# Turning the softmax probabilities of four heads by VectorE block transposes and small transfers instead of TensorE transposes, in one decoder layer on one core

## The chip, the cores and the metric

The kernel runs on one core of a Trainium2 chip. The metric is device time in microseconds (us) of one execution. Before the change, three runs gave 305.89 us in the median (305.8 to 306.62). A profiled execution is a run of its own with its own time.

## The reference

One layer of a hybrid decoder trunk on a sequence of 256 tokens with model width 1024, all in float32:

- RMSNorm of x, then one combined input projection. Its columns are the queries, keys and values of 8 attention heads of width 64, and the queries, keys, values, output gate and decay gate of 4 gated-linear-attention heads.
- The attention heads (called MoBA): rotary embedding, then causal softmax attention. A block is 256 keys long and there are 256 tokens, so there are no past blocks to choose from and each query attends causally to its own block.
- The linear-attention heads: a chunked scan, normalised per head and multiplied by silu of the gate.
- Both halves side by side go through the output projection, and x is added.
- Then RMSNorm, an up-projection to 2 x 2816, a causal depthwise convolution of width 3, silu gating, a down-projection, the residual and a last RMSNorm.

## The kernel before, in words

TensorE does every large product in three passes: each float32 operand is split into a rounded part `hi` and a rest `lo`, and the kernel adds hi x hi, hi x lo and lo x hi. ScalarE makes `hi` (line 99), VectorE makes `lo = raw - hi` (line 102). Weights come through a ring of four raw buffers. `split_lo` (line 101) calls `load_next` when a slot of weights is fully split, so the load of a later slot is issued by SyncE (SP) right behind that subtraction.

The input projection is a list of 48 numbered steps (line 121). From step 24 on, a step is one contraction block of 128 for a group of 512 columns and both token halves: six matrix products of 512 columns. Steps 24 to 31 make the values of attention, 32 to 39 those of the linear heads, 40 to 47 the output gate; the output projection follows as steps 48 to 63. Weight slots 12 and 13 serve steps 32 to 39, slots 14 and 15 serve steps 40 to 47 (two steps to each half of a slot), slots 16 to 19 the output projection.

All other work is written out by hand in a table (lines 631 to 653): for a step, or for the middle of a step (36.5 is between the two token halves of step 36), it lists the calls that are emitted there. TensorE, ScalarE and VectorE each run their instructions strictly in the order in which they are emitted; SyncE and GpSimd run theirs in order too. So a call placed in the table at one step stands in one place in three or four queues.

The attention heads are done in pairs, one pair per "visit", at steps 29, 33.5, 36.5 and 40. A visit of pair `pr` has these parts:

- `m_scores(pr)` (line 526): TensorE makes the scores of both heads in two PSUM tiles, and with them one level of the linear heads (`lvl_c`).
- `m_max(h)` (line 553): VectorE adds the causal mask, writes into a 448-wide tile `pe` and takes the maximum of each row. Columns 0 to 127 of a head's tile belong to its first 128 queries, columns 128 to 383 to its last 128, with 64 queries in each half of the rows (in the second group the two halves are swapped).
- `m_exp(h)` (line 561): ScalarE takes the exponential and its row sum.
- `m_div(h)` (line 568): VectorE takes the reciprocals, ScalarE scales the 128 columns of the first part, VectorE the 256 of the second.
- `m_pt(pr)` (line 574): one visit later, TensorE turns the probabilities of the pair with 12 transposes into PSUM, and ScalarE copies them out to `pt` with four instructions (lines 587 and 588).

At step 45.5 everything comes together: `m_pt(3)`, the last level of the linear heads (`lvl_last`, copied out by ScalarE in `lvl_last_d`), `m_av(0)` (heads 0 to 3 times values, line 591), `m_av(1)` (heads 4 to 7), and `g_av(0)`, `g_av(1)` for the linear heads. Then steps 46 and 47 finish the projection, `g_tail` at step 48 normalises the linear heads, and `g_out` at step 51 transposes them on TensorE.

Late in the kernel the same idea as in the change is already used once: `blocks` (line 910) turns 32 x 32 blocks on VectorE and `to_rows` (line 916) puts the blocks in their places with 16 transfers from the SP queue.

Of the kernel before, what the change touches and what calls it, by code (L numbers as in the profile page):

```python
# [26 lines left out]
NG = 256 + RANK + 256  # L27
# [7 lines left out]
def trunk_kernel(ctx: ExitStack, tc: tile.TileContext, xT_d, wG_d, w5_d, wo_d, up_d, dn_d,  # L35
                 par_d, gla_g_d, fin_g_d, wgu_d, cos_d, sin_d, causal_d, lvl_d, ident_d, out_d):
    nc = tc.nc
    V, A, T, DMA = nc.vector, nc.scalar, nc.tensor, nc.sync
# [123 lines left out]
    ml = main.tile([128, KT, S], F32R, name="ml")  # L162
# [43 lines left out]

    ap_ = ctx.enter_context(ExitStack())
    at = ap_.enter_context(tc.tile_pool(name="attn", bufs=1))
    gqk = at.tile([128, 2, NG], F32, name="gqk")
    gqT = at.tile([128, 2, S], F32, name="gqT")  # L210
    gkT = at.tile([128, 2, S], F32, name="gkT")
    gk1 = at.tile([128, 2, S], F32, name="gk1")
    q1 = at.tile([128, 256], F32, name="q1")
    dec = [at.tile([128, 512 >> i], F32, name=f"dec{i}") for i in range(7)]
    q128 = at.tile([128, 2, 64], F32, name="q128")
    k128 = at.tile([128, 2, 64], F32, name="k128")
    ATd = at.tile([128, 8, 64], F32, name="ATd")
    AT = at.tile([128, 8, 128], F32, name="ATf")
    AT01 = at.tile([128, 4, 128], F32, name="AT01")
    wgs = at.tile([128, 256], F32R, name="wgs")  # L220
    lrs = at.tile([128, 2, 8, RANK], F32R, name="lrs")
    lrT = at.tile([128, S], F32R, name="lrT")
# [6 lines left out]
    gv = at.tile([128, 2, 512], F32, name="gv")  # L229
# [8 lines left out]
    st = {}  # L238
# [198 lines left out]
        st["last"] = p  # L437

    def lvl_last_d():
        for h in range(2):  # L440
            p = st["last"][h]
            for a in range(2):
                A.activation(AT.rearrange("p (a g h) t -> p a g h t", a=2, h=2)[0:64, a, :, h, 64:128],
                             p[HALVES[a], 0:128].rearrange("p (g t) -> p g t", g=2), AF.Copy)
            A.activation(AT01.rearrange("p (a h) t -> p a h t", h=2)[:, :, h],
                         p[:, 128:384].rearrange("p (a t) -> p a t", a=2), AF.Copy)
# [7 lines left out]
    def g_av(tt):  # L454
        p = att()
        for h in range(HG):
            pr, hh = divmod(h, 2)
            o = p[:, h * DV:(h + 1) * DV]
            vs = slice(h * DV, (h + 1) * DV)
            if tt == 1:  # L460
                T.matmul(o, AT01[:, pr * 2 + hh], gv[:, 0, vs], start=True, stop=False)
            i = (pr * 2 + tt) * 2 + hh
            T.matmul(o, AT[:, i], gv[:, tt, vs], start=(tt == 0), stop=True)  # L463
        st["o", tt] = p
# [81 lines left out]

    pes = [at.tile([128, 448], F32, name=f"pe{i}") for i in range(4)]
    for pe in pes:  # L550
        nc.gpsimd.memset(pe[64:128, 384:448], 0.0)

    def m_max(h):
        p, pe = st["s", h], pes[h % 4]
        mx = at.tile([128, 8], F32, name="mx", bufs=4)
        for i, (a, b, c) in enumerate(((0, 128, 0), (64, 320, 128))):
            V.tensor_tensor_reduce(pe[:, c:c + b - a], p[:, a:b], causal[:, c:c + b - a], -(HD ** -0.5), 3e38,
                                   ALU.add, ALU.min, mx[:, i:i + 1])
        st["mx", h] = mx

    def m_exp(h):
        pe, mx = pes[h % 4], st["mx", h]
        for i, (a, b) in enumerate(((0, 128), (128, 384))):
            A.activation(pe[:, a:b], pe[:, a:b], AF.Exp, bias=mx[:, i:i + 1], scale=-1.0,
                         accum_out=mx[:, 4 + i:5 + i])
        st["pe", h] = pe

    def m_div(h):
        mx, pe = st["mx", h], st["pe", h]
        V.reciprocal(mx[:, 6:8], mx[:, 4:6])  # L570
        A.activation(pe[:, 0:128], pe[:, 0:128], AF.Copy, scale=mx[:, 6:7])
        V.tensor_scalar(pe[:, 128:384], pe[:, 128:384], mx[:, 7:8], None, op0=ALU.mult)

    def m_pt(pr):

        p = [att() for _ in range(2)]
        for h in range(2):
            for c in range(3):
                for r, rs in enumerate(HALVES):
                    a = c * 128 + 64 * (r and c > 0)  # L580
                    T.transpose(p[r][:, (3 * h + c) * 64:(3 * h + c) * 64 + 64],  # L581
                                st["pe", 2 * pr + h][rs, a:a + 128], ident[rs, rs])
        pt = at.tile([128, 2, 384], F32, name="pt", bufs=4)
        for r in range(2):
            o = pt.rearrange("p h (c t) -> p h c t", c=3)
            i = p[r][:, :384].rearrange("p (h c t) -> p h c t", h=2, c=3)
            A.activation(o[:, :, 0, HALVES[r]], i[:, :, 0], AF.Copy)
            A.activation(o[:, :, 1:, HALVES[1 - r]], i[:, :, 1:], AF.Copy)
        st["pt", pr] = pt

    def m_av(n):

        p = att()
        for pr in (2 * n, 2 * n + 1):
            c = S * (pr % 2)
            for hh in range(2):
                h = 2 * pr + hh
                pt = st["pt", pr][:, hh]
                r = slice(64 * hh, 64 * hh + 64)
                vs = slice(64 * h, 64 * h + 64)  # L600
                T.matmul(p[r, c:c + S], mv[:, 0, vs], pt[:, 0:256], start=True, stop=False, skip_group_check=True)  # L601
                T.matmul(p[r, c + 128:c + 256], mv[:, 1, vs], pt[:, 256:384],
                         start=False, stop=True, skip_group_check=True)
        mh = st["mh"]
        pv = p.rearrange("p (a t) -> p a t", a=2)
        A.activation(mh[:, 2 * n:2 * n + 2], pv, AF.Copy)
        V.tensor_sub(ml[:, 2 * n:2 * n + 2], pv, mh[:, 2 * n:2 * n + 2])


    plan = {}  # L610
# [20 lines left out]
    for q, f in (  # L631
# [78 lines left out]
    for q, (g, k) in enumerate(steps):  # L710
# [6 lines left out]
        n, kk = where[g, k]  # L717
        h_, l_ = slots[n].view(512 if g else NG)
        if g in (1, 2):
            for pr in range(4):  # L720
# [3 lines left out]
                o = st[names[g]][pr // 2][:, (pr % 2) * S:(pr % 2 + 1) * S]  # L724
# [39 lines left out]
    for q in range(48, 64):  # L764
        ph, j = divmod(q - 48, 8)
# [409 lines left out]
```

## Time and profile before

| | |
|---|---|
| Median of three runs | 305.89 us (305.8 to 306.62) |
| The profiled execution's own time | 306.11 us |
| Span of its instructions | 304.1 us |
| TensorE busy | 297.7 us (98%) |
| VectorE busy | 248.2 us (82%) |
| ScalarE busy | 207.0 us (68%) |
| GpSimd busy | 4.8 us (2%) |

The span runs from the first to the last instruction of the program; 2.0 us of the execution's own time lie outside it. Busy shares are averages over the whole span. Steps 33.5 to 48, where the change is made, lie at 57 to 91 us of it. In the rows of the trace the first number is the start in us from the beginning of the span and the second the duration; "L581" is line 581 of the kernel; "x12" counts instructions that were merged in one row, and "[0.64 <-ACT hi L99]" says that the engine stood idle for 0.64 us before the row until that instruction released it.

### The profile page before, as it was taken

To read this page: it belongs to the slowest core of one execution; us is meant where nothing else is said; L and a number is where in the kernel's file an instruction comes from. 1 tells how busy PE (TensorE), PEld (TensorE's weight loads), DVE (VectorE), ACT (ScalarE), POOL (GpSimd) and SP (SyncE) were. 2 spreads that over 40 slices of the span, in tenths; PEclk is the share of its full clock that TensorE was granted. 3 is DMA by queue.
4 is the path that set the end of the run, shared out by engine and by line. 5 is a ranking of instruction groups with operands and counts; after the bars stand their busy time and mean duration, and the time that the engine had idled before them with its cause. 6 is when DMAs were issued, how large, how long until landed. Compare 5 with 4: busy or idle time off the path is not lost.

```text
span 304.1 us, 6224 instructions
## 1 busy us (share of the span) xinstructions
PE 297.7 (98%) x2470; PEld 282.2 (93%) x2470; DVE 248.2 (82%) x464; ACT 207.0 (68%) x384; POOL 4.8 (2%) x21
## 2 busy tenths in 40 slices
PE   8999999999999999999999999999999999999992
PEld 8999988777889999999999999999999999999992
DVE  3788998999387699799999998887888788876653
ACT  3988999898998487657667775555556665534362
POOL 2020000000000000000000000000000000000000
PEclk9999999999999999999999999999999999999999
DMA  6998845274553542991567666448788622220003
GB/s 163 391 332 307 297 165 198 91 261 141 176 182 134 204 168 65 426 370 32 210 245 256 254 235 236 170 156 224 211 194 234 267 71 69 71 69 2 0 0 139
DMA packets 20892, 56.38 MB, mean 185 GB/s; under 512 B 9840, under 2 KB 11648, under 8 KB 16640
## 3 DMA queue, kind: packets, MB, share of 16 engines
q1 hardware_dynamic: 20720, 55.86, 53.1%
q8 instruction: 19, 0.31, 0.4%
q10 hardware_dynamic: 144, 0.13, 0.1%
q14 instruction: 9, 0.07, 0.1%
HBM read 53.89 MB, written 1.05 MB: 181 GB/s over the span
## 4 chain that ended last, share of the span: by engine, by line
PE 98%; ACT 0%; issue 0%; DVE 0%; ACTq 0%
PE att L116 14%; PE att L117 14%; PE att L118 14%; PE acc L116 14%; PE acc L118 14%; PE acc L117 14%; PE att L746 4%; PE acc L727 1%; PE att L77 1%; PE att L399 1%; PE att L535 1%; PE att L581 1%; PE att L463 1%; PE att L601 1%; PE acc L735 1%; PE att L302 0%
## 5 line engine op out<-in xcount | busy, mean ns | idle before, releaser
L99 ACT ACTIVATE hi<-raw 128x1024 fp32r<-128x1024 f32 (+4 forms) x87 | 79.9, 941 | 38.4 <-PE att L117 31.9
L102 DVE TENSOR_TENSOR lo<-raw,hi 128x1024 fp32r<-128x1024 f32 (+4 forms) x89 | 93.6, 1065 | 14.0 <-ACT hi L99 14.0
L116 PE MATMUL att<-hh,hi 128*128 128x256 f32 x352 | 98.4, 279 | 0.0
L117 PE MATMUL att<-hl,hi 128*128 128x256 f32 x352 | 98.3, 279 | 0.0
L118 PE MATMUL att<-hh,lo 128*128 128x256 f32 x352 | 98.2, 279 | 0.0
L116 PEld LDWEIGHTS att<-hh,hi 128*128 128x128 f32 x352 | 66.2, 188 | 0.0
L117 PEld LDWEIGHTS att<-hl,hi 128*128 128x128 f32 x352 | 66.2, 188 | 0.0
L118 PEld LDWEIGHTS att<-hh,lo 128*128 128x128 f32 x352 | 66.2, 188 | 0.0
L873 DVE SCALAR_TENSOR_TENSOR c<-us,par,c 128x256 f32<-128x256 f32 x88 | 40.7, 482 | 4.1 <-ACT c L865 2.5
L865 ACT ACTIVATE c<-us,par 128x256 f32<-128x256 f32 x44 | 24.0, 591 | 23.7 <-DVE us L855 18.4
L118 PE MATMUL acc<-dhi,gl 128*128 128x512 f32 (+1 forms) x88 | 32.1, 365 | 0.0
L117 PE MATMUL acc<-dlo,gh 128*128 128x512 f32 (+1 forms) x88 | 32.1, 365 | 0.0
L116 PE MATMUL acc<-dhi,gh 128*128 128x512 f32 (+1 forms) x88 | 31.9, 363 | 0.0
L815 DVE TENSOR_TENSOR dlo<-draw,dhi 128x1024 fp32r<-128x1024 f32 x22 | 26.6, 1218 | 0.0
L855 DVE TENSOR_TENSOR us<-att,rb 128x512 f32<-128x512 f32 x20 | 13.8, 688 | 11.5 <-PE att L118 11.5
L810 ACT ACTIVATE dhi<-draw 128x1024 fp32r<-128x1024 f32 x22 | 23.0, 1046 | 0.0
L116 PE MATMUL acc<-hi,ah 128*128 128x512 f32 x48 | 19.5, 406 | 0.0
L118 PE MATMUL acc<-hi,al 128*128 128x512 f32 x48 | 19.0, 396 | 0.0
L117 PE MATMUL acc<-lo,ah 128*128 128x512 f32 x48 | 19.0, 396 | 0.0
L117 PEld LDWEIGHTS acc<-dlo,gh 128*128 128x128 f32 x88 | 16.5, 188 | 2.0
L116 PEld LDWEIGHTS acc<-dhi,gh 128*128 128x128 f32 x88 | 16.5, 188 | 1.9
L118 PEld LDWEIGHTS acc<-dhi,gl 128*128 128x128 f32 x88 | 16.5, 188 | 1.9
(222 smaller groups left out, 511.0 us busy)
## 6 DMA issues: line engine op xcount, KB each, us to landing
raw<-in_up SPq DMA_DIRECT2D x22, 1024.0 KB, 4.9
draw<-in_dn SPq DMA_DIRECT2D x22, 512.0 KB, 5.7
raw<-in_w SPq DMA_DIRECT2D x7, 1024.0 KB, 6.8
raw<-in_wo SPq DMA_DIRECT2D x4, 1024.0 KB, 4.8
raw<-in_w SPq DMA_DIRECT2D x4, 512.0 KB, 5.6
raw<-in_wG SPq DMA_DIRECT2D x3, 528.0 KB, 5.8
raw<-in_w SPq DMA_DIRECT2D x4, 256.0 KB, 5.4
xg<-hB SPq DMA_DIRECT2D x16, 64.0 KB, 6.4
```

Of the source, the lines that this page charges most:

```text
L77: T.matmul(wp[:, :w], zero, zero[:, :w], start=True, stop=True)
L99: A.activation(self.hi[:, a:b], self.raw[:, a:b], AF.Copy)
L102: V.tensor_sub(self.lo[:, a:b], self.raw[:, a:b], self.hi[:, a:b])
L116: T.matmul(out, sh, mh, start=first, stop=False, **kw)
L117: T.matmul(out, sh, ml, start=False, stop=False, **kw)
L118: T.matmul(out, sl, mh, start=False, stop=last, **kw)
L746: T.matmul(st["G"][tt][c][:, :c1 - c0], sta[:, k, tt * 128:(tt + 1) * 128], mov[:, kk, c0:c1], start=k == 0 and i == 0, stop=k == KT - 1 a ...
L810: A.activation(hi, downs[i][0], AF.Copy)
L815: V.tensor_sub(lo, d, hi)
L855: V.tensor_tensor(u[:, :, 2:], upo[i][2].rearrange("p (a t) -> p a t", a=2), rb[:, None, :].to_broadcast([128, 2, S]), op=ALU.mult)
L865: A.activation(cv[i][:, a], u[:, a, 2:], AF.Identity, bias=par[:, P_CB + m:P_CB + m + 1], scale=par[:, P_CW + 2 * 2 * NP + m:P_CW + 2 * 2 ...
L873: V.scalar_tensor_tensor(c[:, a], u[:, a, w:w + S], par[:, wc:wc + 1], c[:, a], op0=ALU.mult, op1=ALU.add)
```

## The change

Heads 0 to 3 no longer go through `m_pt`. Their four probability tiles become one tile `pe4`. Once the third visit has issued its work, `p_blocks` transposes all 32 x 32 blocks of `pe4` with two VectorE instructions into `tb`, which takes the memory of `gqk`; the second instruction overwrites, for token rows 64 to 127, the blocks whose order differs. Then `p_turn` places the blocks in `pt4` with twenty transfers, taken in turn by the SP queue and the GpSimd queue: 12 that move 32 x 12 pieces of 128 bytes and 8 that move 32 x 4. `m_av(0)` reads `pt4`.

What goes with it: heads 4 and 5 use two buffers of another tile group (`e`), heads 6 and 7 the first two quarters of `pe4` again. For heads 2 to 5 the second scaling of `m_div` moves from VectorE to ScalarE. `m_pt(0)` and `m_pt(1)` are gone. At step 36.5, `lo(14, 1)` now comes behind `lvl_d_(4)`, `p_blocks` and `p_turn`. `lo(15, 0)` moves from step 37 to the fourth visit, behind `m_exp(7)`, and the fourth visit moves from step 40 to 40.5. The columns of `m_av(0)` come out in another order, so its copies (ScalarE) and subtractions (VectorE) are three instructions each instead of one. `AT01` takes the memory of `gk1`, and `pt` needs two buffers instead of four.

```diff
-    gqk = at.tile([128, 2, NG], F32, name="gqk")
+    gqk = at.tile([128, 2, NG], F32, name="gqk", tag="gqk")
...
-    pes = [at.tile([128, 448], F32, name=f"pe{i}") for i in range(4)]
-    for pe in pes:
-        nc.gpsimd.memset(pe[64:128, 384:448], 0.0)
+    pe4 = at.tile([128, 4, 448], F32, name="pe4")
+    nc.gpsimd.memset(pe4[64:128, :, 384:448], 0.0)
+
+    def pe_of(h):
+        if h not in (4, 5):
+            return pe4[:, h % 4 if h < 4 else h - 6]
+        if ("pe", h) not in st:
+            st["pe", h] = at.tile([128, 512], F32, name="e", bufs=2)
+            nc.gpsimd.memset(st["pe", h][64:128, 384:448], 0.0)
+        return st["pe", h]
+
+    pt4 = at.tile([128, 12, 128], F32, name="pt4")
+    nc.gpsimd.memset(pt4.rearrange("p (h c) t -> p h c t", c=3)[64:128, :, 2, 64:128], 0.0)
+
+    def p_blocks():
+        st["tb"] = at.tile([128, 50, 32], F32, name="tb", tag="gqk")
+        t = st["tb"][:, 0:48].rearrange("p (h n) b -> p h (n b)", h=4)
+        V.transpose(t, pe4[:, :, 0:384])
+        V.transpose(t[64:128, :, 64:192], pe4[64:128, :, 0:128])
+
+    def p_turn():
+        n = 0
+        for b in range(4):
+            j = b // 2
+            for k in range(4):
+                src = st["tb"][32 * b:32 * b + 32]
+                dst = pt4[32 * k:32 * k + 32, :, 32 * b:32 * b + 32]
+                o = k + 2 * j
+                whole = j == 0 or k < 2
+                for c in ((None,) if whole else (0, 1)):
+                    q = (DMA, nc.gpsimd)[n % 2]
+                    n += 1
+                    if c is None:
+                        q.dma_start(dst, src[:, o:o + 45:4])
+                    else:
+                        q.dma_start(dst[:, c::3], src[:, o + 4 * c:o + 4 * c + 37:12])
...
-        V.tensor_scalar(pe[:, 128:384], pe[:, 128:384], mx[:, 7:8], None, op0=ALU.mult)
+        if h in (2, 3, 4, 5):
+            A.activation(pe[:, 128:384], pe[:, 128:384], AF.Copy, scale=mx[:, 7:8])
+        else:
+            V.tensor_scalar(pe[:, 128:384], pe[:, 128:384], mx[:, 7:8], None, op0=ALU.mult)
...
-                pt = st["pt", pr][:, hh]
+                pt = pt4[:, 3 * h:3 * h + 3].rearrange("p c t -> p (c t)") if n == 0 else st["pt", pr][:, hh]
...
-        A.activation(mh[:, 2 * n:2 * n + 2], pv, AF.Copy)
-        V.tensor_sub(ml[:, 2 * n:2 * n + 2], pv, mh[:, 2 * n:2 * n + 2])
+        for a, b, c in ((0, 256, 0),) if n else ((0, 128, 0), (128, 192, 192), (192, 256, 128)):
+            A.activation(mh[:, 2 * n:2 * n + 2, a:b], pv[:, :, c:c + b - a], AF.Copy)
+        for a, b, c in ((0, 256, 0),) if n else ((0, 128, 0), (128, 192, 192), (192, 256, 128)):
+            V.tensor_sub(ml[:, 2 * n:2 * n + 2, a:b], pv[:, :, c:c + b - a], mh[:, 2 * n:2 * n + 2, a:b])
...
-            (33.5, lambda: do((hi, 13, 1), (m_scores, 1), (m_pt, 0), (m_max, 2), (m_exp, 2), (m_max, 3), (m_exp, 3), (lvl_u, 4), (m_div, 2), (m_div, 3), (lo, 13, 1), (lvl_d_, 3), (mv_evac, 0), (mv_evac, 1), (hi, 14, 0), (lo, 14, 0))),
-            (36.5, lambda: do((hi, 14, 1), (m_scores, 2), (m_pt, 1), (m_max, 4), (m_exp, 4), (m_max, 5), (m_exp, 5), (lvl_u, 5), (m_div, 4), (m_div, 5), (lo, 14, 1), (lvl_d_, 4))),
-            (37, lambda: do((hi, 15, 0), (lo, 15, 0))),
-            (40, lambda: do((hi, 15, 1), (m_scores, 3), (m_pt, 2), (m_max, 6), (m_exp, 6), (m_max, 7), (m_exp, 7), (lvl_u64,), (lvl_d_, 5), (m_div, 6), (m_div, 7), (lvl_join,), (lo, 15, 1))),
+            (33.5, lambda: do((hi, 13, 1), (m_scores, 1), (m_max, 2), (m_exp, 2), (m_max, 3), (m_exp, 3), (lvl_u, 4), (m_div, 2), (m_div, 3), (lo, 13, 1), (lvl_d_, 3), (mv_evac, 0), (mv_evac, 1), (hi, 14, 0), (lo, 14, 0))),
+            (36.5, lambda: do((hi, 14, 1), (m_scores, 2), (m_max, 4), (m_exp, 4), (m_max, 5), (m_exp, 5), (lvl_u, 5), (m_div, 4), (m_div, 5), (lvl_d_, 4), (p_blocks,), (p_turn,), (lo, 14, 1))),
+            (37, lambda: do((hi, 15, 0))),
+            (40.5, lambda: do((hi, 15, 1), (m_scores, 3), (m_pt, 2), (m_max, 6), (m_exp, 6), (m_max, 7), (m_exp, 7), (lo, 15, 0), (lvl_u64,), (lvl_d_, 5), (m_div, 6), (m_div, 7), (lvl_join,), (lo, 15, 1))),
```

More of the change, by code (lines that the diff above doesn't have):

```diff
@@ L208, in trunk_kernel @@
     at = ap_.enter_context(tc.tile_pool(name="attn", bufs=1))
-    gqk = at.tile([128, 2, NG], F32, name="gqk")
+    gqk = at.tile([128, 2, NG], F32, name="gqk", tag="gqk")
     gqT = at.tile([128, 2, S], F32, name="gqT")
     gkT = at.tile([128, 2, S], F32, name="gkT")
-    gk1 = at.tile([128, 2, S], F32, name="gk1")
+    gk1 = at.tile([128, 2, S], F32, name="gk1", tag="gk1")
     q1 = at.tile([128, 256], F32, name="q1")
@@ L218, in trunk_kernel @@
     AT = at.tile([128, 8, 128], F32, name="ATf")
-    AT01 = at.tile([128, 4, 128], F32, name="AT01")
     wgs = at.tile([128, 256], F32R, name="wgs")
@@ L439, in lvl_last_d @@
     def lvl_last_d():
+        AT01 = st["AT01"] = at.tile([128, 4, 128], F32, name="AT01", tag="gk1")
         for h in range(2):
@@ L460, in g_av @@
             if tt == 1:
-                T.matmul(o, AT01[:, pr * 2 + hh], gv[:, 0, vs], start=True, stop=False)
+                T.matmul(o, st["AT01"][:, pr * 2 + hh], gv[:, 0, vs], start=True, stop=False)
             i = (pr * 2 + tt) * 2 + hh
@@ L545, in masks @@
             nc.gpsimd.tensor_copy(causal[rs, 320:384], causal[rs, rs])
-    pes = [at.tile([128, 448], F32, name=f"pe{i}") for i in range(4)]
-    for pe in pes:
-        nc.gpsimd.memset(pe[64:128, 384:448], 0.0)
+    pe4 = at.tile([128, 4, 448], F32, name="pe4")
[30 more added lines that the diff above has]
+                        q.dma_start(dst[:, c::3], src[:, o + 4 * c:o + 4 * c + 37:12])
     def m_max(h):
-        p, pe = st["s", h], pes[h % 4]
+        p, pe = st["s", h], pe_of(h)
         mx = at.tile([128, 8], F32, name="mx", bufs=4)
@@ L561, in m_exp @@
     def m_exp(h):
-        pe, mx = pes[h % 4], st["mx", h]
+        pe, mx = pe_of(h), st["mx", h]
         for i, (a, b) in enumerate(((0, 128), (128, 384))):
@@ L582, in m_pt @@
                                 st["pe", 2 * pr + h][rs, a:a + 128], ident[rs, rs])
-        pt = at.tile([128, 2, 384], F32, name="pt", bufs=4)
+        pt = at.tile([128, 2, 384], F32, name="pt", bufs=2)
         for r in range(2):
```

## The prediction

> **What bounds the kernel now.** I read the page's busy shares first, then the chain of work that ended last, then the queues of TensorE, VectorE and ScalarE in order of time from 57 to 96 us, and last the transfers.
>
> ```profile
> span 304.1 us, 6224 instructions
> PE 297.7 (98%) x2470; PEld 282.2 (93%) x2470; DVE 248.2 (82%) x464; ACT 207.0 (68%) x384; POOL 4.8 (2%) x21
> PE 98%; ACT 0%; issue 0%; DVE 0%; ACTq 0%
> ```
>
> TensorE is busy for 98% and the chain runs through it from start to end: whatever leaves its queue is gained, as long as nothing that its later instructions wait for comes late. The chain in order of time shows the pieces that the change touches, and that TensorE waits nowhere between them:
>
> ```profile
> 58.57 0.53 PE att L581 x12
> 64.65 0.53 PE att L581 x12
> 71.97 0.43 PE acc L116
> 72.40 0.23 PE acc L117
> 79.87 0.52 PE att L581 x12
> 81.25 0.59 PE att L601 x4
> 82.76 0.43 PE att L601 x4
> 84.06 1.09 PE att L463 x8
> 94.63 0.64 PE att L499 x16
> ```
>
> A product of 512 columns takes 0.23 us, so a step of six takes 1.4 us. `m_pt(0)` and `m_pt(1)` are the first two rows. `m_pt(3)` stands at 79.87, `m_av(0)` at 81.25, `m_av(1)` at 82.76, `g_av(0)` at 84.06, `g_out` at 94.63.
>
> **The change, part by part.** *TensorE* loses 24 transposes: 2 x 0.53 = **-1.06 us**. The scores and the reorderings change nothing in its count. All its work from the third visit on comes 1.06 us earlier if it never waits: `m_pt(3)` at 78.81, `m_av(0)` at 80.2, `m_av(1)` at 81.7, `g_av(0)` at 83.0, `g_out` at 93.6.
>
> *VectorE and ScalarE* must then deliver earlier. VectorE's queue in order of time:
>
> ```profile
> 62.02 0.35 DVE L572 TENSOR_SCALAR pe<-pe,mx 128x256 f32<-128x256 f32 x1
> 65.01 1.23 DVE L102 TENSOR_TENSOR lo<-raw,hi 128x1024 fp32r<-128x1024 f32 x1 [0.64 <-ACT hi L99]
> 68.21 0.35 DVE L572 TENSOR_SCALAR pe<-pe,mx 128x256 f32<-128x256 f32 x1
> 68.57 0.17 DVE L570 RECIPROCAL mx<-mx 128x2 f32<-128x2 f32 x1
> 69.05 1.22 DVE L102 TENSOR_TENSOR lo<-raw,hi 128x1024 fp32r<-128x1024 f32 x1
> 70.18 0.50 DVE L410 COPY_PREDICATED ATd<-lvl,att 128x128 f32<-128x128 int32 x2
> 74.49 0.16 DVE L570 RECIPROCAL mx<-mx 128x2 f32<-128x2 f32 x1
> 78.98 2.36 DVE L102 TENSOR_TENSOR lo<-raw,hi 128x1024 fp32r<-128x1024 f32 x2 [2.34 <-ACT hi L99]
> 91.81 1.29 DVE L491 TENSOR_TENSOR y<-y,gr 128x512 f32<-128x512 f32 x2 [0.18 <-ACT gr L452]
> ```
>
> ```profile
> 59.32 0.28 ACT L587 ACTIVATE pt<-att 128x128 f32<-128x128 f32 x1
> 60.67 0.50 ACT L564 ACTIVATE pe<-pe,mx 128x256 f32<-128x256 f32 x1
> 61.07 0.18 ACT L564 ACTIVATION_READ_ACCUMULATOR pe<-pe,mx 128x1 f32 x1
> 63.93 2.00 ACT L99 ACTIVATE hi<-raw 128x1024 fp32r<-128x1024 f32 x2
> 74.68 0.87 ACT L571 ACTIVATE pe<-pe,mx 128x128 f32<-128x128 f32 x2
> 77.89 1.99 ACT L99 ACTIVATE hi<-raw 128x1024 fp32r<-128x1024 f32 x2
> 80.42 0.28 ACT L587 ACTIVATE pt<-att 128x128 f32<-128x128 f32 x1 [0.53 <-PE att L581]
> 81.29 0.56 ACT L443 ACTIVATE ATf<-att 64x128 f32<-64x128 f32 x2
> 92.24 2.00 ACT L99 ACTIVATE hi<-raw 128x1024 fp32r<-128x1024 f32 x2
> ```
>
> From 65.0 on VectorE stands in an unbroken row until after the reciprocals of heads 6 and 7 (74.49); its next idle time is the 2.34 us before 78.98. So what is added ahead of 74.49 arrives there in full:
>
> 1. *Scalings of heads 2 and 3 to ScalarE.* A 256-wide instruction holds ScalarE 0.40 us (60.67 to 61.07), two hold it 0.8. The copies of `m_pt(0)` that go (from 59.32) don't pay for it, because the exponentials behind them wait for VectorE's maxima anyway. So `hi(14, 0)` moves from 63.93 to about 64.65, and `lo(14, 0)`, which already waited 0.64 us for it, comes later by **+0.7**; VectorE's own saving of two scalings is lost in that wait.
> 2. *Scalings of heads 4 and 5:* VectorE saves about 0.25 each net of latencies, **-0.5**. ScalarE pays with the dropped copies of `m_pt(1)`.
> 3. *Block transposes.* Their only rows are the ones used late in the kernel:
>
> ```profile
> L913 DVE STREAM_TRANSPOSE hB<-xg x4: 703/704/707, 175.3 to 199.1; 128x512 f32<-128x512 f32 x4
> ```
>
> 512 columns cost 0.70; a subtraction of 1024 columns costs 1.22, so each further 512 cost 0.53. The first instruction has 4 x 384 = 1536 columns: 0.70 + 2 x 0.53 = 1.76. The second has 512: 0.70. Less two overlaps of 0.1: **+2.3**.
>
> The reciprocals of heads 6 and 7 so move by 0.7 - 0.5 + 2.3 = 2.5 us, from 74.49 to 77.0. (`lo(15, 0)` stands ahead of them before and after.) Weights still come in time: `lo(14, 1)` now ends at 70.27 + 0.7 - 0.5 + 0.4 (`lvl_d_(4)` goes first) + 2.3 = 73.2, and step 42 wants it at 73.9 (71.97 + 0.2 + 2 x 1.4 - 1.06); `lo(15, 0)` ends near 75.4, wanted at 76.7. The first margin is only 0.7 us.
>
> Behind the reciprocals ScalarE stands, in order: two scalings, `lvl_join`, `gv_evac`, `hi(16, 0)`, `hi(16, 1)`, then the copies of `m_pt(3)`. Before, this took from 74.68 to 79.88 (5.2 us), and ScalarE then still waited 0.53 us for TensorE. After: 77.2 + 5.2 = 82.4, copies of 0.87 us (80.42 to 81.29), ready at 83.3. `m_av(1)` wants them at 81.7. TensorE waits **+1.6 us** there. `g_av(0)` then comes at 84.6; its copies (`lvl_last_d`, 1.4 us from 81.29 in the old queue, now from 83.3) end at 84.7, the same moment. `g_out` comes at 94.63 + 0.54 = 95.2; its input ended at 93.1 (91.81 + 1.29) and is delayed by at most the 1.9 us of ScalarE's copies, 95.0. No further wait. The three-piece copies of `m_av(0)` cost ScalarE and VectorE some 0.1 to 0.2 us inside that slack.
>
> 4. *Twenty transfers.* `m_av(0)` reads all of them. `p_blocks` starts where `lvl_d_(4)`, now first, ends: 69.05 + 0.7 - 0.5 + 0.4 = 69.65, and ends at 72.0. Because `m_av(1)` waits until 83.3 and `m_av(0)` needs 1.5 (81.25 to 82.76), landings until **81.8** cost nothing more; each us beyond is a us lost.
>
> ```profile
> L920 SPq DMA_DIRECT2D xg<-hB x16: 597/720/847, 202.2 to 229.2; - x16
> 50.37 0.33 SPq L92 DMA_DIRECT2D raw<-in_w  x1
> 58.95 18.08 SPq L92 DMA_DIRECT2D raw<-in_wo  x4
> 201.31 0.33 SPq L92 DMA_DIRECT2D raw<-in_up  x1
> 201.69 0.42 SPq L804 DMA_DIRECT2D draw<-in_dn  x1
> 202.16 3.01 SPq L920 DMA_DIRECT2D xg<-hB  x4
> xg<-hB SPq DMA_DIRECT2D x16, 64.0 KB, 6.4
> out_y<-yy SPq DMA_DIRECT2D x3, 128.0 KB, 1.9
> raw<-in_wo SPq DMA_DIRECT2D x4, 1024.0 KB, 4.8
> L690 POOL CAST identr<-ident 128x128 fp32r<-128x128 f32 x1 | 1.6, 1637 | 16.1 <-DMA ident<-in_ident 16.1
> ```
>
> SP took 0.72 us to issue 16 x 32 = 512 pieces and 0.33 us to issue the 128 rows of a weight slot; in proportion 384 pieces take 0.59. SP's half is 6 x 0.59 + 4 x 0.33 = 4.9 us, issued by 76.9. Landing took 1.9 us for the stores at the end, and 6.4 where a weight slot and a tile of down-weights had been issued just ahead (201.31, 201.69). Here the load ahead is that of slot 17, issued behind `lo(13, 1)` near 64 and landed 4.8 us later, so I take 1.9: 78.8. With 6.4 it would be 83.3. The load for slot 18 is queued behind them on SP, from about 73 to 77, and lands by 82; ScalarE splits that slot after 92 (the last of the ScalarE rows). GpSimd's queue holds nothing behind its ten that is wanted before the FFN, past 100 us.
>
> GpSimd issues no transfer in this trace. Below, its price can't be less than SP's, 0.49 on average; above, I take its slowest instruction, 1.64 us. The landing then is between 78.8 and 72.0 + 16.4 + 1.9 = 90.3: between +0.5 and **+9.0 us** in the sum. The row nearest in kind is SP's issue of the same kind of pieces, so the forecast takes that; GpSimd stays free up to 0.79 us on average (81.8 - 72.0 - 1.9 over ten).
>
> The Trainium skill, "DMA: Bandwidth & Descriptors", section "Anatomy of one DMA — SWDGE (gpsimd) path", speaks against the change: a transfer issued from GpSimd carries about 2 us of fixed cost, mostly completion rather than issue. Ten that overlap would by it keep the forecast; ten one behind the other would give an estimate of 72 + 21 = 93, about +12 us. No run here shows such a transfer yet.
>
> **Sum:** -1.06 + 1.6 = +0.54 on the profiled execution's 306.11 us, 306.65. That execution lay 0.2 above the runs' median (305.89), so **306.4 us**. A measurement of this kernel can tell about 0.3%, 0.92 us, from no change.
>
> **The rivals.** *GpSimd late:* its software issue is slower than 0.79 us a transfer, TensorE stops at `m_av(0)`, and the change is slower. At the mean of the two bounds, (0.49 + 1.64)/2 = 1.06, the last lands at 84.5 and the sum is 0.54 + 2.7 = +3.2: 309.1 us; at the upper bound 314.9. For it: two-dimensional pieces of 128 bytes and ten in a row on an engine whose plain 128-wide cast took 1.64 us. Against: SP does the same for 0.72. It decides from 82.2 on (0.92 - 0.54 beyond 81.8).
>
> *All of TensorE's gain is kept:* ScalarE isn't late, because the transposes are cheaper or the queue behind the reciprocals has slack that I didn't see. -1.06: 304.8 us. For it: VectorE's 2.34 us of idle time just behind. Against: this slack lies behind the reciprocals, and ScalarE was idle only 0.53 us.
>
> *The work removed isn't on the path:* TensorE's products behind the transposes are paced by weights and the 1.06 us reappear there; with the wait for ScalarE then shortened to 0.5, about +0.5, again no change. Against: the chain has no wait at 58 or 64 us.
>
> **How the numbers follow.** Forecast 0.45, GpSimd late 0.41, gain kept 0.09, not on the path 0.05. The two likeliest are nearly even, since the price of GpSimd's issue is the one term without a row. The forecast's own range is 305.6 to 307.0 (0.7 either way from the durations). The whole range reaches to GpSimd's middle and somewhat beyond, and to just above the gain kept: 305.3 to 311.0. Faster: the gain kept and 0.01 of the forecast's lower tail, 0.10. Same: not on the path and 0.40 of the forecast, 0.45. Slower: GpSimd late and 0.04 of the forecast's upper tail, 0.45.
>
> **What would show it.** Right: no transposes of probabilities behind the scores of the second and third visit (58 and 64 us); VectorE's two transposes near 1.8 and 0.7 us from about 69.7; the reciprocals of heads 6 and 7 near 77; ScalarE's copies of `m_pt(3)` at 82 to 83; TensorE's one gap of 1.6 us ahead of `m_av(1)`. Wrong: a gap ahead of `m_av(0)` that ends with a transfer; a gap at step 42 (the 0.7 us margin); GpSimd's issues longer than 0.79 us; no gap at all and a span near 303.

## The result, and the profile after

The changed kernel takes **309.41 us** in the median (307.77 to 310.19); the kernel before, beside it, 305.97 us. The ratio is 1.0102, with a 95% interval of 1.0072 to 1.0133: slower by 3.1 us. The forecast was 306.4 us; the time lies inside the range to 311.0, but not for the reason that the range was opened for: GpSimd wasn't late. That it lies inside is luck.

The profiled execution took 309.44 us. The head of its page:

```profile
span 307.7 us, 6219 instructions
PE 297.8 (97%) x2446; PEld 282.0 (92%) x2446; DVE 249.7 (81%) x464; ACT 207.0 (67%) x382; POOL 11.0 (4%) x31
PE 77%; ACT 9%; DVE 8%; issue 3%; DMA 1%; SPq 0%; DVEq 0%; ACTq 0%
```

TensorE has 24 instructions fewer (2446 for 2470) and yet is as busy as before, 297.8 for 297.7 us: some of its other work took longer. The chain that ended last, which was TensorE for 98%, now runs through ScalarE for 9% and VectorE for 8%. TensorE's queue around `m_av(0)` (lines 637 and 638 of the changed kernel; `m_pt` is line 617):

```profile
78.27 0.59 PE L617 MATMUL att<-ident,pe 64*128 64x64 f32 x12
...
82.65 0.66 PE L637 MATMUL att<-pt,mv 128*64 128x256 f32 x4 [2.92 <-ACT pt L624]
...
84.11 1.18 PE L637 MATMUL att<-pt,mv 128*64 128x256 f32 x4
...
86.92 1.32 PE L463 MATMUL att<-gv,ATf 128*128 128x128 f32 x8
```

Two things stand here. TensorE is idle for 2.92 us ahead of **`m_av(0)`**, until ScalarE's copy in line 624, which is a copy of `m_pt(3)`. And the products of `m_av(1)` then take 1.18 us for four where the same four took 0.66 us a moment before. The windows view (columns: window, its length, busy time and instructions of TensorE, weight loads, VectorE, ScalarE, GpSimd, then the granted clock of TensorE, the busy share of the DMA engines and GB/s) has the reason in the column of the clock:

```profile
79.00:82.00 3.00, 0.73 (x48) 0.59 (x42) 0.74 (x1) 3.00 (x5) 0.10 (x1) 1.00 0.81 252
82.00:84.00 2.00, 1.35 (x15) 1.18 (x17) 1.62 (x2) 1.98 (x9) 0.00 (x0) 0.97 0.97 406
84.00:86.00 2.00, 2.00 (x17) 1.75 (x15) 0.63 (x3) 1.29 (x6) 0.00 (x0) 0.50 1.01 401
86.00:88.00 2.00, 2.00 (x16) 1.59 (x13) 0.54 (x2) 0.97 (x2) 0.00 (x0) 0.68 0.87 360
88.00:90.00 2.00, 2.00 (x20) 2.00 (x19) 1.75 (x3) 2.00 (x7) 0.00 (x0) 1.00 0.09 33
```

The clock was 1.00 through the idle time, 0.50 from about 83.9 to 87.3 us, and 1.00 again. In the kernel before it is 1.00 in all these windows, for instance:

```profile
84.00:86.00 2.00, 2.00 (x19) 2.00 (x19) 1.34 (x3) 1.91 (x3) 0.00 (x0) 1.00 0.75 311
```

Not every execution of the changed kernel seems to have this fall. 3.4 us at half clock lower the mean granted clock of an execution by 0.0055. Four of the six runs have a mean clock of 0.989 to 0.991 and took 309.39 to 310.19 us; the other two have 0.994 and 0.995, where the runs of the kernel before lie too (0.994 to 0.999), and took 308.35 and 307.77 us. Only one execution was profiled, so this is read from the mean clocks alone.

Where the 3.55 us between the two spans (304.10 and 307.65) lie, by the starts of TensorE's instructions in the two traces (for its last product, the end):

| stretch | before | after | difference |
|---|---|---|---|
| start to the first visit (step 29) | 48.74 | 48.26 | -0.48 |
| to `m_pt(3)` | 31.06 | 30.01 | **-1.05** |
| `m_pt(3)` to `m_av(0)` | 1.39 | 4.38 | **+2.99** |
| `m_av(0)` to `g_av(0)` | 2.80 | 4.27 | **+1.47** |
| `g_av(0)` to TensorE's last product | 214.53 | 214.70 | +0.17 |
| to the end of the span | 5.58 | 6.03 | **+0.45** |

The first row is work that the change doesn't touch; it lay between 48.3 and 49.1 us in the profiles of this study, so nothing is read from it. The gain of the removed transposes is there in full. Three losses eat it: the idle time, the halved clock behind it, and something at the end of the program.

VectorE's queue, which the forecast had followed:

```profile
69.17 1.77 DVE L566 STREAM_TRANSPOSE tb<-pe 128x1536 f32<-128x1536 f32 x1
70.97 0.71 DVE L567 STREAM_TRANSPOSE tb<-pe 64x512 f32<-64x512 f32 x1
71.71 1.23 DVE L102 TENSOR_TENSOR lo<-raw,hi 128x1024 fp32r<-128x1024 f32 x1
...
73.96 1.22 DVE L102 TENSOR_TENSOR lo<-raw,hi 128x1024 fp32r<-128x1024 f32 x1
...
76.77 0.16 DVE L603 RECIPROCAL mx<-mx 128x2 f32<-128x2 f32 x1
```

And ScalarE's, from the scalings of heads 6 and 7 to the copies of `m_pt(3)`:

```profile
76.96 0.88 ACT L604 ACTIVATE pe<-pe,mx 128x128 f32<-128x128 f32 x2 [1.91 <-DVE mx L603]
77.86 0.63 ACT L417 ACTIVATE ATf<-ATd 64x512 f32<-64x512 f32 x1
78.50 0.63 ACT L418 ACTIVATE ATf<-ATd 64x512 f32<-64x512 f32 x1
79.04 1.24 ACT L449 ACTIVATE gv<-acc,rsx 128x512 f32<-128x512 f32 x2
80.18 1.99 ACT L99 ACTIVATE hi<-raw 128x1024 fp32r<-128x1024 f32 x2
82.07 0.26 ACT L623 ACTIVATE pt<-att 128x128 f32<-128x128 f32 x1
82.23 0.37 ACT L624 ACTIVATE pt<-att 128x256 f32<-128x256 f32 x1
```

ScalarE waits 1.91 us for the reciprocals, then has 5.1 us of work in an unbroken row ahead of the copies; the first two copies end at 82.60, and TensorE starts 0.05 us later. The pair frees one of the four PSUM tiles, and that tile is the one that `m_av(0)` writes.

The transfers, from the view of the tile `pt` (columns: line, queue, count; minimum, median and maximum ns of an issue; first and last start):

```profile
L582 SPq DMA_DIRECT2D pt<-tb x6: 599/620/1090, 71.0 to 76.2; - x6
L582 POOL DMA_DIRECT2D pt<-tb x6: 615/617/739, 71.2 to 75.5; - x6
...
L584 POOL DMA_DIRECT2D pt<-tb x4: 548/556/560, 74.4 to 76.7; - x4
L584 SPq DMA_DIRECT2D pt<-tb x4: 599/612/624, 74.9 to 77.5; - x4
...
DMA to landing us min/median/max: 1.9/2.7/3.7
```

GpSimd issues as quickly as SP. All landed by 78.8 us, except the last one of SP, at 81.16. TensorE doesn't take up so many waits at once: its sequencer has nine semaphore instructions ahead of `m_av(0)`, 0.05 us each and 0.107 us apart. Their starts, from the sequencer's records in the trace (semaphores 102 to 110 are those of SP's transfers, 111 to 118 those of GpSimd's):

```
changed kernel   79.32 79.43 79.54 79.64 79.75 | 81.19 81.30 81.40 81.51   (the sixth waits for 107 and 113)
x_both           79.86 79.97 80.07 80.18 80.28 80.39 80.50 80.60 80.71
x_touch          73.58 73.69 73.80 73.91 74.12 74.23 74.38 74.49 74.59
```

So in the changed kernel two things end close together: the transfers with their waits at 81.56 us, and ScalarE's copies at 82.60. The later one is named in the trace; the experiments ask whether it is really the one that decides, and what is left once it is gone.

### The profile page after: what moved, and what is told of

The parts are those of the page before. It is cut to its first block, busy times and chain, and to the rows that moved or that the text cites. A ratio compares the mean times of both kernels' runs of the same rounds, so it can differ in the third digit from the quotient of the medians.

```text
span 307.7 us, 6219 instructions
## 1 busy us (share of the span) xinstructions
PE 297.8 (97%) x2446; PEld 282.0 (92%) x2446; DVE 249.7 (81%) x464; ACT 207.0 (67%) x382; POOL 11.0 (4%) x31
## 3 DMA queue, kind: packets, MB, share of 16 engines
HBM read 53.89 MB, written 1.05 MB: 179 GB/s over the span
## 4 chain that ended last, share of the span: by engine, by line
PE 77%; ACT 9%; DVE 8%; issue 3%; DMA 1%; SPq 0%; DVEq 0%; ACTq 0%
PE att L116 14%; PE att L117 14%; PE att L118 14%; PE acc L116 9%; PE acc L117 9%; PE acc L118 9%; PE att L784 3%; DVE lo L102 3%; ACT hi L99 3%; ACT qs L512 2%; PE acc L765 1%; DMA raw<-in_w 1%; PE att L637 1%; DVE ATd L409 1%; DVE pe L590 1%
```

## The experiments

Two theories stood at the start. **A, late copies:** VectorE's added work makes the reciprocals of heads 6 and 7 late, ScalarE's queue passes that on to the copies of `m_pt(3)`, and these hold a PSUM tile that `m_av(0)` needs. **B, late transfers:** `m_av(0)` waits for the twenty transfers, whatever the trace names. A third claim stood beside them: the halved clock follows from TensorE's idle time.

**x_blocks: the changed kernel without its transfers.** The tile `pt4` is zeros, so the turned probabilities of heads 0 to 3 are left out of the result.

```diff
-    nc.gpsimd.memset(pt4.rearrange("p (h c) t -> p h c t", c=3)[64:128, :, 2, 64:128], 0.0)
+    nc.gpsimd.memset(pt4, 0.0)
...
-(lvl_d_, 4), (p_blocks,), (p_turn,), (lo, 14, 1)
+(lvl_d_, 4), (p_blocks,), (lo, 14, 1)
```

> The changed kernel with the two VectorE block instructions but without the twenty transfers; m_av(0) multiplies a pt4 that holds only zeros, so the turned probabilities of heads 0 to 3 are left out. Theory A (late copies): the block instructions make the reciprocals of heads 6 and 7 2.3 us later, ScalarE's copies of m_pt(3) end late, and m_av(0) waits for the PSUM tile that the first of these copies frees, at about 82.6 us. Then the transfers are not what holds TensorE: the gap of about 2.9 us ahead of m_av(0) stays, the granted clock dips behind it, and the time stays at 308 to 310. Theory B (late transfers): the last landing at 81.2 us and the waits of TensorE on it hold m_av(0); without transfers the gap goes and the time is 305 to 306.

310.52 us, ratio 1.0125 (1.0079 to 1.0171). TensorE's row at `m_av(0)`, and the granted clock behind it:

```profile
83.34 1.13 PE L637 MATMUL att<-pt,mv 128*64 128x256 f32 x4 [2.89 <-ACT pt L624]
```

```profile
82.00:84.00 2.00, 0.66 (x4) 0.48 (x6) 2.00 (x2) 1.99 (x7) 0.00 (x0) 0.54 0.93 393
84.00:86.00 2.00, 2.00 (x17) 1.54 (x15) 0.30 (x1) 1.35 (x5) 0.00 (x0) 0.50 0.35 74
86.00:88.00 2.00, 2.00 (x15) 1.54 (x13) 0.82 (x3) 0.72 (x3) 0.00 (x0) 0.50 0.92 385
```

With no transfer at all the gap is 2.89 us, against 2.92. Theory B falls as the cause of this gap; what makes it is the copies. The clock stayed at 0.50 for 6.8 us here (82.2 to 89.0), twice as long as in the changed kernel, and the time is longer though work is left out.

**x_busy: the gap filled.** Ten products of zeros keep TensorE at work behind `lvl_last`; all else as changed.

```diff
+        for n in range(10):
+            T.matmul(p[0][:, 384:512], zero, zero, start=True, stop=True)
         st["last"] = p
```

> The changed kernel with ten products of zeros (128 columns) on TensorE behind lvl_last, into columns of its PSUM tile that nobody reads: TensorE works through most of the gap of 2.9 us. Theory C (clock): the slow products behind the gap (clock 0.50 at 84 to 86 us) come from TensorE standing idle; kept busy, it holds full clock, m_av(0) still begins near 82.6, and the time falls by about 1.5 us to 307.4 to 308.2, with every run at a mean clock above 0.998. Rival: the clock falls for another reason (the weight loads that land then, the step of load after it); then the time stays at 309 to 310.

308.16 us, ratio 1.0074 (1.0059 to 1.0089).

```profile
80.32 2.50 PE L437 MATMUL att<-const-float32-0.0 128*128 128x128 f32 x20
83.28 0.66 PE L639 MATMUL att<-pt,mv 128*64 128x256 f32 x4 [0.47 <-ACT pt L626]
```

```profile
82.00:84.00 2.00, 1.53 (x18) 1.21 (x17) 2.00 (x2) 1.99 (x7) 0.00 (x0) 1.00 0.94 369
84.00:86.00 2.00, 2.00 (x28) 1.78 (x24) 0.25 (x1) 1.91 (x8) 0.00 (x0) 1.00 1.03 385
```

`m_av(0)` comes no earlier (4.35 us behind `m_pt(3)`, which stands at 78.93; 4.38 in the changed kernel), but the clock stays at 1.00, and from `m_av(0)` to `g_av(0)` it takes 2.80 us as in the kernel before, for 4.27. Of the 3.4 us lost, 1.25 are gone by the medians and 0.9 by the ratios. All four runs of x_busy have a mean clock of 0.996 to 0.998, and their times (307.90 to 308.43 us) are those of the two runs of the changed kernel whose mean clock isn't lowered. The halved clock comes from the idle time, and idle time of this length can cost more than itself.

**x_second: the turning moved one visit earlier.** `p_blocks` and `p_turn` stand behind `lvl_d_(3)` in the second visit, so VectorE's 2.5 us no longer lie between the reciprocals of the third visit and the maxima of the fourth, and the transfers start some 6 us earlier.

```diff
-(lo, 13, 1), (lvl_d_, 3), (mv_evac, 0)
+(lo, 13, 1), (lvl_d_, 3), (p_blocks,), (p_turn,), (mv_evac, 0)
...
-(lvl_d_, 4), (p_blocks,), (p_turn,), (lo, 14, 1)
+(lvl_d_, 4), (lo, 14, 1)
```

> The changed kernel with the block instructions and the transfers behind the second visit (after lvl_d_(3)) instead of the third: VectorE stood idle there for 1.9 us. All work is done. Theory A: the reciprocals of heads 6 and 7 come at about 74.9 instead of 76.8, ScalarE's copies of m_pt(3) begin at about 80.3, and m_av(0) waits about 1 us for the first pair of them; no dip of the clock; 305.5 to 306.5. Theory B: transfers that land by about 75 free m_av(0) at 79.7; the whole gain of 1.06 us is seen: 304.6 to 305.2.

306.01 us, ratio 1.0004 (0.9994 to 1.0014).

```profile
80.81 0.66 PE L637 MATMUL att<-pt,mv 128*64 128x256 f32 x4 [0.86 <-ACT pt L624]
```

3.4 us of loss are gone, but the gain doesn't appear.

**x_both: ScalarE's queue mended as well.** In the fourth visit the scalings of heads 6 and 7 come ahead of the second-last level of the linear heads; `lvl_join` moves to step 42, and `hi(16, 1)`, `lo(16, 1)` behind `m_av(1)`.

```diff
-(lo, 15, 0), (lvl_u64,), (lvl_d_, 5), (m_div, 6), (m_div, 7), (lvl_join,), (lo, 15, 1)
+(lo, 15, 0), (m_div, 6), (m_div, 7), (lvl_u64,), (lvl_d_, 5), (lo, 15, 1)
...
-(42, lambda: do((hi, 16, 1), (lo, 16, 1))),
+(42, lambda: do((lvl_join,))),
...
-(m_av, 0), (m_av, 1), (g_av, 0)
+(m_av, 0), (m_av, 1), (hi, 16, 1), (lo, 16, 1), (g_av, 0)
```

> As the run with the transfers behind the second visit, and with another order: the scalings of heads 6 and 7 ahead of lvl_u64 and lvl_d_(5), lvl_join at step 42 behind gv_evac and hi(16, 0), and hi(16, 1), lo(16, 1) behind m_av(1). All work is done. Theory A: nothing is left that makes the copies of m_pt(3) late; m_av(0) begins without a wait and the 24 transposes are gained in full: 304.6 to 305.3. Theory B: the same as the run without the new order, 304.6 to 305.2 in both. If the gain of 1.06 us is not on the path at all, 305.7 to 306.2.

305.93 us, ratio 0.9996 (0.9986 to 1.0005). Neither expectation reached its number. TensorE and ScalarE at this place:

```profile
80.81 0.66 PE L637 MATMUL att<-pt,mv 128*64 128x256 f32 x4 [0.55 <-ACT pt L624]
```

```profile
79.53 0.25 ACT L623 ACTIVATE pt<-att 128x128 f32<-128x128 f32 x1
79.69 0.36 ACT L624 ACTIVATE pt<-att 128x256 f32<-128x256 f32 x1
```

The gap is still put down to line 624, but that copy was done at 80.05, 0.76 us before `m_av(0)` started, and the last transfer had landed at 75.03. What ends at 80.76 is the row of nine semaphore instructions shown above. With the 0.45 us at the end of the program they make 1.0 us, which is the whole gain.

**x_order: the same order, the transfers left at the third visit.** It has x_both's edits of the order, of which the first is repeated here, without those of x_second:

```diff
-(lo, 15, 0), (lvl_u64,), (lvl_d_, 5), (m_div, 6), (m_div, 7), (lvl_join,), (lo, 15, 1)
+(lo, 15, 0), (m_div, 6), (m_div, 7), (lvl_u64,), (lvl_d_, 5), (lo, 15, 1)
...
```

> The changed kernel with only ScalarE's order mended: the reciprocals and scalings of heads 6 and 7 ahead of the second-last level of the linear heads, lvl_join at step 42, hi(16, 1) and lo(16, 1) behind m_av(1). The transfers stay at the third visit. If late copies of m_pt(3) were all that held m_av(0), the gap ahead of it shrinks to about 0.6 us as in x_both, and the time is about 306 us. If the transfers of the third visit would have held it next (the last one landed at 81.2 us in the changed kernel, and the last of TensorE's waits on them ended at 81.6), m_av(0) starts near 81.6 instead of 82.65, the gap is about 2 us, and the time is 307.5 to 308.4 us, by whether the clock still dips.

306.37 us, ratio 1.0006 (0.9997 to 1.0015).

```profile
81.35 0.66 PE L637 MATMUL att<-pt,mv 128*64 128x256 f32 x4 [1.29 <-DMA pt<-tb]
```

Once the copies are early, the transfers are what TensorE waits for, and theory B's mechanism is real as the next one in line. It costs less than expected (1.29 us, not 2): the last one landed at 80.89 and the waits were through at 81.29. At 1.29 us of idle time the clock stays at 1.00. ScalarE's order alone brings back 3 of the 3.4 us that were lost.

**x_sp: x_both with all twenty transfers on SP.**

```diff
-                    q = (DMA, nc.gpsimd)[n % 2]
+                    q = DMA
```

> x_both with all twenty transfers on the SP queue, none on GpSimd. Theory: GpSimd's eight transfer semaphores cost 0.45 us at the end of the program (5.58 to 6.03 us from TensorE's last product to the end of the span) and are about half of the nine waits of 0.1 us each on TensorE ahead of m_av(0). Then the end is back at 5.6 us, four or five waits are left, the gap ahead of m_av(0) is 0.1 to 0.3 us, and the time is 305.1 to 305.3 us. Rival: the longer end and the waits come from twenty transfers more, whoever issues them; the time stays at 305.9 us.

306.17 us, ratio 0.9998 (0.9987 to 1.0009): a miss, but not one for the rival.

```profile
81.80 0.66 PE L637 MATMUL att<-pt,mv 128*64 128x256 f32 x4 [1.20 <-ACT AT L445]
```

TensorE's waits are down to five, as expected, but one queue needs from 65.95 to 80.34 us to issue twenty transfers, and the last lands at 81.56, so the gap is longer. The end of the program shrinks only from 6.03 to 5.91 us with no transfer on GpSimd, so GpSimd's semaphores as such aren't its cause.

**x_early and x_best: `m_av(0)` between wide products.** x_early is x_both with `m_av(0)` at step 44.5; x_best has the transfers on SP alone as well.

```diff
+            (44.5, lambda: do((m_av, 0),)),
...
-(m_av, 0), (m_av, 1), (hi, 16, 1)
+(m_av, 1), (hi, 16, 1)
```

> x_both with m_av(0) moved from the list of step 45.5 to step 44.5, between products of 512 columns, when all transfers have landed. Theory: TensorE's sequencer takes the nine waits while the wide products ahead of them still run, so the gap of 0.55 us goes; 305.4 us, with the end still 0.45 us longer. Rival: the nine waits stop the queue wherever they stand; 305.9 us, and a gap of 0.5 us at the new place.

305.85 us, ratio 0.9995 (0.9986 to 1.0005). The gap is gone:

```profile
77.28 0.40 PE L118 MATMUL acc<-hi,al 128*128 128x512 f32 x1
77.60 0.66 PE L637 MATMUL att<-pt,mv 128*64 128x256 f32 x4
...
79.10 0.50 PE L116 MATMUL acc<-hi,ah 128*128 128x512 f32 x1
```

The sequencer took the nine waits from 74.0 to 75.5 us. But from the scores of the second visit to `g_av(0)` the trace has 26.18 us, and x_both 26.19. What was gained is paid elsewhere: `m_av(0)` takes 1.50 us here for 1.33 in the block of small products, 0.09 more are lost ahead of it and 0.10 behind it, `m_pt(3)` to `m_av(1)` takes 1.58 us where x_both without its gap takes 1.45, and `m_av(1)` takes 1.50 for 1.45. Why these products take longer there isn't shown.

> Both: transfers on SP alone and m_av(0) at step 44.5. Theory: nothing is left of the 0.55 and 0.45 us, so the 1.06 us of the transposes are gained in full: 304.9 us. Rival: the waits and the longer end stay; 305.4 to 305.9 us.

310.13 us, ratio 1.0119 (1.0092 to 1.0145), a miss by 5 us.

```profile
80.52 1.13 PE L637 MATMUL att<-pt,mv 128*64 128x256 f32 x4 [2.85 <-DMA pt<-tb]
```

```profile
78.00:80.50 2.50, 0.00 (x0) 0.01 (x1) 2.31 (x3) 1.78 (x3) 0.00 (x0) 0.90 0.33 46
80.50:82.50 2.00, 1.98 (x12) 1.56 (x14) 0.00 (x0) 0.00 (x0) 0.00 (x0) 0.50 0.70 258
```

SP's transfers land at 80.25, some 2.6 us later than the moved `m_av(0)` wants them. The expectation hadn't added up SP's 20 x 0.6 us. The run is of use all the same: an idle time of 2.85 us is followed by the halved clock with another cause behind it. Here the clock fell at 80.0 us (a mean of 0.90 in the first window), while TensorE still waited.

**x_tail: x_both with one transfer more on GpSimd.** The end of the program depends on which semaphore the last store signals. SP's transfers take eight semaphores in turn, and at the end SP waits for all of them in a fixed order, 0.06 us each. Ten transfers more turn the last store from 109, with one wait behind it, to 102, with seven.

```diff
-                    q = (DMA, nc.gpsimd)[n % 2]
+                    q = (DMA, nc.gpsimd)[n % 2 or n == 18]
```

> x_both with one of the twenty transfers moved from the SP queue to GpSimd (9 and 11 instead of 10 and 10). Theory of the longer end: SP's transfers signal eight semaphores in rotation (102, 103, 104, 105, 107, 108, 109, 110), and at the end SP waits for them in a fixed order, 0.06 us each. Before, the last store signals 109 and one wait stands behind it; ten more transfers turn that to 102, with seven waits behind it. With nine more the last store signals 110, with none behind it. Then the end is 6.03 - 7 x 0.06 = 5.6 us from TensorE's last product, the gap ahead of m_av(0) stays at 0.55 us, and the time is 305.5 us. Rival: the longer end comes from GpSimd's eight semaphores as such; it stays at 6.0 us, and the time at 305.9.

305.25 us, ratio 0.9974 (0.9963 to 0.9985). The issue of the last store in the kernel before (span 304.10 us):

```profile
301.14 0.45 SPq L1107 DMA_DIRECT2D out_y<-yy  x1
```

in the changed kernel (307.65 us):

```profile
304.24 0.45 SPq L1145 DMA_DIRECT2D out_y<-yy  x1
```

and in x_tail (303.47 us):

```profile
300.42 0.45 SPq L1145 DMA_DIRECT2D out_y<-yy  x1
```

From the store to the end it is 2.96, 3.41 and 3.05 us; from TensorE's last product 5.58, 6.03 and 5.68. The last store of x_tail signals 110, the last semaphore in the row, as expected, and the gap ahead of `m_av(0)` is unchanged, 0.56 us. In x_sp the last store signals 104, with five waits behind it: two fewer than in x_both, and the end is 0.12 us shorter, two waits of 0.06. With no wait behind it x_tail's end is still 0.1 us longer than that of the kernel before, which has one; this rest isn't explained. Against x_both the two ratios make 0.7 us; the trace accounts for 0.35 of it, and the intervals, 0.3 us either way for each, hold the rest.

**x_gather and x_win: one instruction to gather the waits.** A small GpSimd copy of 48 columns of `pt4` onto themselves, behind the last transfer; x_win adds x_tail's edit.

```diff
+        nc.gpsimd.tensor_copy(pt4[:, :, 0::32], pt4[:, :, 0::32])
```

> x_both with one small instruction of GpSimd behind the last transfer, which copies 48 of pt4's columns onto themselves and so waits for all twenty transfers in TensorE's place. Theory: m_av(0) then waits for that one instruction, TensorE's queue loses its nine waits of 0.11 us, the gap of 0.55 us ahead of m_av(0) goes, and the time is 305.4 us. Rival: the gap has another cause than the waits, or TensorE keeps them beside the new one; the gap stays and the time is 305.9 us.

> x_gather and x_tail together. Theory: both costs are gone and the 1.06 us of the transposes are left; 305.0 us, faster than the kernel before by about 1 us. Rival: as much as either of them leaves, 305.4 to 305.9 us.

305.82 us (ratio 0.9991, 0.9982 to 1.0000) and 305.51 us (0.9980, 0.9971 to 0.9988). x_gather is a miss: `m_av(0)` kept nine waits beside the new instruction, and the gap is 0.55 us as before. x_win is as x_tail.

**x_touch: x_tail with an early first reader.** One product of zeros with eight columns of `pt4`, at the start of step 45.

```diff
+    def m_touch():
+        T.matmul(att()[:, 0:8], zero, pt4[:, 0:2, 0::32], start=True, stop=True)
...
+            (45, lambda: do((m_touch,),)),
```

> x_tail with one added product of TensorE at the start of step 45: zeros times eight columns of pt4, into a PSUM tile that nothing reads. It is TensorE's first reader of pt4, so the nine waits on the transfers should stand ahead of it, where twelve products of 512 columns still have to run and TensorE's sequencer is ahead of them (in x_early it took the waits from 74.0 to 75.5 us, for a product that ran at 77.6). Theory: the nine waits are the gap of 0.56 us ahead of m_av(0); they are hidden, the gap is 0 to 0.1 us, the added product costs 0.1 to 0.25 us, and the time is 304.8 to 304.9 us. Rival: m_av(0) keeps its waits, or the gap has another cause; 305.3 us or more.

**304.99 us**, ratio 0.9964 (0.9950 to 0.9978): faster than the kernel before by 1.1 us (0.7 to 1.5), and so than the changed one by some 4 us.

```profile
77.76 0.28 PE L587 MATMUL att<-pt,const-float32-0.0 128*128 128x8 f32 x2
77.90 0.48 PE L116 MATMUL acc<-hi,ah 128*128 128x512 f32 x1
...
78.76 0.59 PE L620 MATMUL att<-ident,pe 64*128 64x64 f32 x12
...
80.15 0.66 PE L640 MATMUL att<-pt,mv 128*64 128x256 f32 x4
```

There is no gap any more: 1.39 us from `m_pt(3)` to `m_av(0)`, as in the kernel before. The added product takes 0.14 us until the next one starts. The nine waits, at 73.6 to 74.6 us, were taken while wide products ahead of them still ran. This shows that they were the 0.55 us, which x_early had only made likely.

The ladder in the end: 1.06 us are gained by the transposes; the profiled execution of the changed kernel loses 3.0 us by the idle time, 1.5 by the clock and 0.45 at the end; in x_both the first is 0.6 and the second nothing; x_touch leaves 0.3 in all, 0.1 of it at the end. By the trace x_touch should gain 0.75 us; the measured 1.1 has that inside its interval. What is left between them may be the time ahead of the first visit, which differed from profile to profile by up to 0.9 us, and stays open.

## Why the prediction was right or wrong

The time fell inside the stated range by luck. The range reached so far up for GpSimd's sake, which was priced at 309.1 us; three losses that the sum didn't have, or had too small, brought the kernel to nearly the same number.

- **The gain of 1.06 us:** right; 1.05 us from the first visit to `m_pt(3)`. The rival by which it is not on the path falls.
- **VectorE's terms:** right. Its two transposes were priced 1.76 and 0.70 and took 1.77 and 0.71 us; the reciprocals were due at 77.0 and stand at 76.77. `lo(14, 1)` ended at 72.9 (due at 73.2) and `lo(15, 0)` at 75.2 (75.4); step 42 doesn't wait.
- **ScalarE's queue:** right. The copies of `m_pt(3)` were due from 82.4 to 83.3 and ran from 82.07 to 83.03, 5.1 us of work behind the reciprocals where the forecast took 5.2.
- **"`m_av(1)` wants them at 81.7. TensorE waits +1.6 us there":** this step failed. The forecast followed the data that `m_av(1)` reads, and not the memory that `m_av(0)` writes. `m_av(0)` needs a PSUM tile; all four were in use, two by `m_pt(3)` and two by `lvl_last`, and the first to come free is one of `m_pt(3)`, through the very copies that were known to be late. So the lateness stands at `m_av(0)`, whose 1.4 us can't be done meanwhile: 2.99 us, not 1.6. x_blocks shows that this alone makes the gap. The gap that the forecast named as its sign, ahead of `m_av(1)`, isn't there. The sentence that landings until 81.8 cost nothing rests on the same error.
- **Left out of the sum, the clock:** in the profiled execution 2.92 us of idle time were followed by 3.4 us at half clock, +1.47. The forecast priced a stall at its length. Whether the 1.6 us that it had would have led to this too is open: 1.29 us (x_order) didn't, 2.85 did, no idle time between them was measured, and in x_blocks the clock fell 1.7 us after TensorE had gone idle (80.45 to 82.2).
- **Left out of the sum, the end:** +0.45 us. The forecast took each transfer's issue and landing as its whole price. Ten more on SP also turned the order in which the end of the program finds its semaphores.
- **Twenty transfers, GpSimd's price:** the forecast's choice was right: 0.62 and 0.56 us, inside the 0.79 that it left free and between the bounds of 0.49 and 1.64. The rival *GpSimd late*, which held 0.41 of the chances and opened the range to 311.0, is wrong as a mechanism. The Trainium skill, "DMA: Bandwidth & Descriptors", section "Anatomy of one DMA — SWDGE (gpsimd) path", gives about 2 us of fixed cost a transfer, mostly completion. GpSimd's ten landed 2.0 to 3.6 us after their issue had begun, SP's ten 1.9 to 3.7, and they overlapped, as the forecast took it.
- **SP's half-size transfers** were priced at 0.33 us, after a weight slot's 128 rows, and took 0.61, as much as the full ones. SP began 1.0 us earlier than forecast (70.96 for 72.0; this profile runs some 0.5 us ahead, and the first transfers need only VectorE's first instruction) and finished 1.2 us later (78.15 for 76.9), and its last transfer landed at 81.16 for 78.8. That was hidden behind the copies and is 1.29 us in x_order. The load of slot 18 behind them was issued at 78.26 and landed at 86.08, not by 82; TensorE didn't wait for it.
- **The waits themselves** weren't priced: "`m_av(0)` reads all of them" is nine instructions in TensorE's queue, 0.96 us if nothing hides them.

The sum was +0.54 us on the profiled execution; in its own terms it missed 1.39 in the stall, 1.47 in the clock, 0.17 behind it and 0.45 at the end, less the 0.48 us by which this profile started earlier: 3.0 us. The forecast had called that no change that a measurement can tell.

## What to carry to other kernels

When an engine that empties PSUM comes late, look for the next instruction that *writes* a tile it holds, and not only for the one that reads its result; the stall stands at the first of the two. Price an idle time of TensorE of some 3 us at its length and, since most executions here paid it, some 1.5 us more for the half clock behind it; fill it or keep it short. A replacement by many small transfers costs its reader one wait for each semaphore pair; let a tiny product early in TensorE's queue be the first reader, while wide products still run, and look at the end of the program too.

## What the runs showed of the hardware

- **Half clock comes in pieces of 3.4 us.** It lasted 3.4 us in the changed kernel (83.9 to 87.3) and in x_best (80.0 to 83.4), and 6.8 us in x_blocks. Idle times of 2.92, 2.89 and 2.85 us led to it in these profiles; 1.29, 1.20 and 0.86 us (x_order, x_sp, x_second) didn't. The length alone doesn't decide: the fall came 1.2 us after the end of the idle time in the changed kernel, but 1.7 (x_blocks) and 2.4 us (x_best) after its start, and by the mean clocks (0.994 to 0.996, for 0.987 to 0.991) it was missing in two of the changed kernel's six runs, in one of x_blocks' four and in two of x_best's six. The Trainium skill, "TensorE: Matmul & The Clock Gate", section "Part 1: The HAM clock gate (the "warmup" mystery)", puts the window at about 3.4 us, which agrees, and asks for an idle window of that length; here less was enough, and the measurement decides.
- **Semaphore instructions on TensorE's queue** stand 0.107 us apart. Behind wide products the sequencer took them ahead of time (74.0 to 75.5 us for a product at 77.6 in x_early, 73.6 to 74.6 for one at 77.8 in x_touch) and so hid them; behind `m_pt(3)` and `lvl_last`, with their products of 64 columns, it didn't (0.55 us idle in x_both).
- **The end of the program** takes 0.06 us for each semaphore that SP still has to wait for behind the one of the last store: 3.05 us from the last store with none behind it (x_tail), 3.41 with seven (the changed kernel).
- **GpSimd issues** a transfer of 384 pieces of 128 bytes in 0.62 us and one of 128 pieces in 0.56, hardly different; SP 0.62 and 0.61. The price here is one for each transfer, not for each piece.
